# Hybrid decoder step on one core: two column groups take turns over the first blocks, with the loads and casts of the start reordered

## The chip, the cores and the metric

The kernel runs on one core of a Trainium2 chip. The metric is the device time of one execution in microseconds (us); lower is better. The time before the change is 1706.85 us, the median of 3 runs (1706.56 to 1708.28).

## The reference, cut to what matters

One layer of a decoder trunk is computed for 256 prompt tokens and 32 sample tokens (8 sequences of 4). The vectors `x` of all 288 tokens (width 2048) meet one wide input projection; its columns feed a short gated convolution and a gated delta-rule mixer. Both results are merged, projected, normalised, and pass through a two-matrix feed-forward part.

```python
proj = x @ w_in                                   # 2048 -> 11280 columns
conv_out, new_conv_a = causal_depthwise_conv(gC * h, conv_a_buf, conv_a_w)
y_a = (gB * conv_out) @ w_a_out
qkv, new_gdn_buf = causal_depthwise_conv(concat([q, k, v]), gdn_buf, gdn_conv_w)
o, S = gated_delta_rule(l2norm(q), l2norm(k), v, g, beta, S0)   # q, k, v after silu
y_b = gated_rmsnorm(o, z) @ w_b_out
x = layer_norm(ALPHA * x + (sig(m_a) * y_a + sig(m_b) * y_b) @ w_o)
x = layer_norm(ALPHA * x + square(relu(x @ w_up)) @ w_down)
```

The sample tokens bring histories: the last convolution inputs of each sequence (`state_conv_a`, `state_gdn_conv`) and the delta-rule state. Everything is in 32-bit floats.

## The kernel before, in words

**Blocks.** Every product with a weight matrix is cut into *column groups* of 256 output columns, and each group into *blocks* of 512 rows of the weight matrix. A block is one DMA of 512 KB (`load`, L164, on SP's queue, into a tile `raw`, 4 buffers). To keep accuracy, each weight and each activation is split into a rounded part and a rest: `split_hi` (L173) casts `raw` to `hi` on ScalarE, `split_lo` (L179) computes `lo` = `raw` - `hi` on VectorE, and `matmuls` (L186) issues 24 matmuls for the block: 4 row tiles, 2 column tiles, and for each the *triple* hi by xh (L202), hi by xl (L203), lo by xh (L204). `hi` and `lo` have 4 buffers each. A group's 4 blocks (with 2048 rows) accumulate in one of two PSUM tiles `acc`; after the group's last block an *evacuation* is spread over the following blocks by `at(...)`.

**Order.** The program writes the order of each engine out by hand; an engine runs its instructions in program order. The main loop (L1309) does, for each block i: the cast `hi` of block i+3 (`AHEAD` = 3), one step of the side work, `lo` of block i+3, the evacuations that are due, the matmuls of block i, and the load of block i+7. While `matmuls` runs, one entry of the list `fill` is emitted after each triple.

**The start.** The first blocks multiply by `x`, which must first be turned: tokens stand on partitions in DRAM's order, and the matmuls want features on partitions. `x` comes as four *parts* of 512 features (`xr[i]`, L715 to L718), prompt (512 KB) and sample tokens (64 KB) by separate DMAs, each followed by `load(i)`, all on SP's queue. `x_tile(k)` (L732) turns 128 features: two transposes of 128x128 for the prompt, a small one for the 32 sample tokens, then a cast to `xh` on ScalarE and the rest `xl` on VectorE. Part 0 is turned before block 0; the tiles of part i+1 are the `fill` of block i (i = 0, 1, 2), and `hi` and `lo` of block i+1 are emitted just ahead of block i. Ahead of all this, 8 bf16 matmuls on a zeroed tile `warm` are issued (L708). The histories, convolution weights and three gain vectors are loaded into `hwr`, `har` (16 DMAs on POOL's queue, from the beginning) and `lnr` (SP's queue), and turned by `hist_tiles` (L741) ahead of block 4. The constants `cf`, `cfe`, `ci`, and `wbar`, `arow` are loaded on SP's queue behind block 4's load (L1285 to L1293).

**The first 24 blocks** are the six groups k, k, q, q, v, v of the delta-rule's first four heads (`conv_evac`, L249). Group 0 has blocks 0 to 3, group 1 blocks 4 to 7. The evacuation of a group has two pieces on successive blocks, each with copies out of PSUM on ScalarE (L263, L264), a multiplication (L266), three fused steps on VectorE (L268) and two small POOL copies, and then a step `last` with the SiLU.

**The side work** is a generator: `gates()` (from block 4), then the delta rule `gdn(0)` (from block 20 at the earliest) and `gdn(1)`, one step per block; a second generator `sample()` runs beside it. Its instructions stand between those of the blocks on every engine.

Of the kernel before, what the change touches and what calls it, by code (L numbers as in the profile page):

```python
# [103 lines left out]
def hybrid_kernel(ctx: ExitStack, tc: tile.TileContext, A):  # L104
# [15 lines left out]
    def nm(s):  # L120
        counter[0] += 1
        return f"{s}{counter[0]}"

    def gtile():
        n = nm("g")
        return gp.tile([P, 512], F32, tag="g", name=n)
# [12 lines left out]
    def tt(out, a, b, op):  # L139
        dve.tensor_tensor(out=out, in0=a, in1=b, op=op)  # L140
# [23 lines left out]
    def load(i):  # L164
        if i >= len(blocks):
            return
        gi, r0, k0, _, _ = blocks[i]
        t = wp.tile([P, KB, GW], F32, tag="raw", name=nm("raw"))
        sp.dma_start(t, gi["W"][r0:r0 + KB * P, gi["col0"]:gi["col0"] + GW]
                     .rearrange("(k p) c -> p k c", p=P))  # L170
        raw[i] = t
# [77 lines left out]
    def conv_evac(sec, G, p):  # L249
        def piece(t):  # L250
            hh = 2 * p + t
            ti = sec * 8 + 4 * G + hh
            tl = {}

            def f(ps):
                gpool = gd["pool"]
                w1 = gpool.tile([P, 640], F32, tag="w1", name=nm("w1"), bufs=2)
                pad, cv = w1[:, 0:320], w1[:, 320:640]
                tl["cv"] = cv
                sm = pad[:, 259:315].rearrange("p (b s) -> p b s", s=7)  # L260
                gps.memset(pad[:, 0:3], 0.0)
                gps.tensor_copy(sm[:, :, 0:3], hw[:, ti, 0:24].rearrange("p (b j) -> p b j", j=3))
                act.copy(pad[:, 3:259], ps[:, t, 0:NP_])  # L263
                act.copy(sm[:, :, 3:7], ps[:, t, NP_:NT].rearrange("p (b s) -> p b s", s=4))  # L264
                c = cv[:, 0:312]
                act.mul(c, pad[:, 0:312], hw[:, ti, 24:25])  # L266
                for j in range(1, 4):
                    stt(c, pad[:, j:j + 312], hw[:, ti, 24 + j:25 + j], c, MUL, ADD)  # L268
                gps.tensor_copy(stB[:, ti, :].rearrange("p (g j) -> p g j", j=3),
                                pad[:, 256:319].rearrange("p (g s) -> p g s", s=7)[:, :, 0:3])  # L270

            def f2(ps):
                cv = tl["cv"]
                cs = cv[:, 259:315].rearrange("p (b s) -> p b s", s=7)[:, :, 0:4]
                if sec == 2:
                    act.activation(gd["v", G][:, hh // 2, :, hh % 2, :],
                                   cv[:, 0:NP_].rearrange("p (c x) -> p c x", c=4), AF.Silu)
                    act.activation(gd["vs", G][:, hh], cs, AF.Silu)
                else:
                    side_ = hh % 2 if sec == 1 else 1 - hh % 2  # L280
                    act.activation(gd["kq", G][:, hh, :, side_, :],
                                   cv[:, 0:NP_].rearrange("p (c x) -> p c x", c=4), AF.Silu)
                    act.activation(gd["kqs", G][:, 1 - sec, hh], cs, AF.Silu)
            return f, f2
        (a0, a1), (b0, b1) = piece(0), piece(1)

        def last(ps):
            a1(ps)
            b1(ps)
        return [a0, b0, last]  # L290

    mark = {}
    for G in range(2):
        mark["kqv", G] = len(blocks)
        for sec, c0 in ((1, C_K), (0, C_Q), (2, C_V)):
            for p in range(2):
                add_group(w_in, c0 + 512 * G + GW * p, 0, KT, acts_x, conv_evac(sec, G, p))
        mark["kqv_end", G] = len(blocks)

    def h_evac(p):  # L300
        def f(ps):
# [403 lines left out]
    warm = tx.tile([P, 512], mybir.dt.bfloat16, name="warm")  # L705
    dve.memset(warm, 0.0)
    wps = gtile()
    for _ in range(8):  # L708
        pe.matmul(wps, warm[:, 0:P], warm, start=True, stop=True)
    xr = [tx.tile([P, 3, 512], F32, name=f"xr{i}") for i in range(4)]  # L710
    xpr = A["x_prompt"][0].rearrange("(b p) f -> p b f", p=P)
    xsr = A["x_sample"].rearrange("b t f -> (b t) f")
    sp.dma_start(cf[:, 0:128], A["cf"][:, 0:128])
    for i in range(4):
        c = slice(512 * i, 512 * i + 512)  # L715
        sp.dma_start(xr[i][:, 0:2, :], xpr[:, :, c])
        sp.dma_start(xr[i][0:NS, 2, :], xsr[:, c])
        load(i)  # L718
    hwr = tx.tile([112, 768], F32, name="hwr")
    har = tx.tile([76, 256], F32, name="har")  # L720
    for g in range(4):
        c, c2 = slice(768 * g, 768 * g + 768), slice(256 * g, 256 * g + 256)
        gps.dma_start(hwr[28 * g:28 * g + 24, :], A["state_gdn_conv"][0].rearrange("b j c -> (b j) c")[:, c])
        gps.dma_start(hwr[28 * g + 24:28 * g + 28, :], A["gdn_conv_w"][0][:, c])
        gps.dma_start(har[19 * g:19 * g + 16, :], A["state_conv_a"][0].rearrange("b j c -> (b j) c")[:, c2])
        gps.dma_start(har[19 * g + 16:19 * g + 19, :], A["conv_a_w"][0][:, c2])
    lnr = tx.tile([33, P], F32, name="lnr")
    gps.memset(epsc[:, 0:1], LN_EPS)
    gps.memset(epsc[:, 1:2], NORM_EPS)
    gps.memset(epsc[:, 2:3], 1.28e-10)  # L730

    def x_tile(k):  # L732
        i, kk = k // 4, k % 4
        g = gtile()
        for b in range(2):
            pe.transpose(g[:, b * P:(b + 1) * P], xr[i][:, b, kk * P:(kk + 1) * P], ident)  # L736
        pe.transpose(g[:, NP_:NT], xr[i][0:NS, 2, kk * P:(kk + 1) * P], ident[0:NS, 0:NS])
        act.copy(xh[:, k, :], g[:, 0:NT])
        tt(xl[:, k, :], g[:, 0:NT], xh[:, k, :], SUB)

    def hist_tiles():  # L741
        g = gtile()
# [529 lines left out]

    cur = [0]
    aux = []
    his[0] = wp.tile([P, KB, GW], F32R, tag="hi", name=nm("hi"))
    los[0] = wp.tile([P, KB, GW], F32R, tag="lo", name=nm("lo"))
    t = raw.pop(0)
    for k in range(KB + 2):
        if k < KB:
            x_tile(k)  # L1280
        if k > 1:
            act.copy(his[0][:, k - 2], t[:, k - 2])  # L1282
            tt(los[0][:, k - 2], t[:, k - 2], his[0][:, k - 2], SUB)
    load(4)
    sp.dma_start(cf[:, 128:], A["cf"][:, 128:NE])  # L1285
    sp.dma_start(cfe, A["cf"][:, NE:NL])
    sp.dma_start(ci, A["ci"])
    sp.dma_start(lnr[0:16, :], A["ln1_g"].rearrange("o (k p) -> (o k) p", p=P))
    sp.dma_start(lnr[16:32, :], A["ln1_b"].rearrange("o (k p) -> (o k) p", p=P))
    sp.dma_start(lnr[32:33, :], A["gdn_norm_w"])  # L1290
    sp.dma_start(wbar, w_in[:, C_BA:C_BA + 16].rearrange("(k p) c -> p k c", p=P))
    sp.dma_start(arow[:, 0, :], A["a_log"].to_broadcast([P, 8]))
    sp.dma_start(arow[:, 1, :], A["dt_bias"].to_broadcast([P, 8]))  # L1293
    for i in range(3):
        split_hi(i + 1, 2)
        split_lo(i + 1, 2)
        load(i + 5)
        fill.extend(lambda k=k: x_tile(k) for k in range(4 * i + 4, 4 * i + 8))
        matmuls(i)
    for i in range(4, AHEAD + 3):  # L1300
        split_hi(i)
        split_lo(i)
        load(i + 4)
    sgen = side()
    gcm = None
    for p in range(8):
        for n, f in enumerate(residual1(p)):
            at(mark["up"] + 6 + 4 * p + n, f)
    for i in range(3, len(blocks)):  # L1309
        cur[0] = i  # L1310
        split_hi(i + AHEAD)
        if i == 4:
            hist_tiles()
            tx_cm.__exit__(None, None, None)
            gcm = tc.tile_pool(name="gdn", bufs=1)
            gpool = gcm.__enter__()
            gd["pool"] = gpool
            for G in range(2):
                gd["kq", G] = gpool.tile([P, 4, 4, 2, 64], F32, tag="kq", name=f"kq{G}", bufs=2)
                gd["kqs", G] = gpool.tile([P, 2, 4, 8, 4], F32, tag="kqs", name=f"kqs{G}", bufs=2)  # L1320
                gd["v", G] = gpool.tile([P, 2, 4, 2, 64], F32, tag="vf", name=f"vf{G}")
                gd["vs", G] = gpool.tile([P, 4, 8, 4], F32, tag="vfs", name=f"vfs{G}")
        if i > 3 and sgen:
            if i == mark["merge"]:
                for _ in sgen:
                    pass
                sgen = None
            else:
                next(sgen, None)
                if aux and next(aux[0], aux) is aux:  # L1330
                    aux.pop(0)
            if i == mark["conv"] + 1:
                gd["ao"] = ap_.tile([P, 2, H, NT], F32, tag="ao", name="ao")
# [24 lines left out]
            tail_consts()  # L1358
        matmuls(i)
        load(i + AHEAD + 4)  # L1360
    for i in sorted(due):
        for f in due[i]:
            f()
# [30 lines left out]
```

## Time and profile before

| what | value |
|---|---|
| median of 3 runs | 1706.85 us (1706.56 to 1708.28) |
| the profiled execution's own time | 1707.81 us |
| its span, first to last instruction | 1706.0 us |
| mean granted TensorE clock | 0.992 |
| TensorE busy (matmul) | 99% of the span |
| VectorE, ScalarE, GpSimd busy | 59%, 43%, 8% |
| DMA moved | 279.69 MB, mean 164 GB/s |

The device time of the profiled execution is 1.81 us longer than its span. "Busy" for TensorE counts an instruction from start to modelled end, so a matmul at half clock counts as busy. Rows of the timeline read: start in us, duration in us, engine, source line, operation, tile written <- tiles read, shape, count, and in brackets how long the engine had been idle and what released it. PE is TensorE, PEld its weight load, ACT ScalarE, DVE VectorE, POOL GpSimd, SP the engine whose queue issues most DMAs; SPq and POOLq are the issuing queues.

### The profile page before, as it was taken

What the parts mean: (1) busy time and instruction counts of PE and PEld (TensorE: products, weight loads), DVE (VectorE), ACT (ScalarE), POOL (GpSimd) and SP (SyncE); (2) the same over time, 40 slices, a digit from 0 to 9 for tenths busy, and PEclk for the clock granted to TensorE, in tenths of its full rate; (3) what the DMA queues carried; (4) which work ended last, traced back from release to release, by engine and by line L of the source; (5) the groups of instructions that cost most, each with busy time, mean ns of one, the idle gap of its engine ahead of it and who ended that gap; (6) DMA issues with size and microseconds to landing.
All of it is one profiled execution on the core that took longest, in us unless ns stands there. A gap on an engine that the chain in (4) does not pass through costs nothing.

```text
span 1706.0 us, 31049 instructions
## 1 busy us (share of the span) xinstructions
PE 1688.2 (99%) x13045; PEld 1668.4 (98%) x13045; DVE 1012.1 (59%) x1301; ACT 726.6 (43%) x1052; POOL 132.4 (8%) x221
## 2 busy tenths in 40 slices
PE   9999999999999999999999999999999999999997
PEld 7999999999999999999999999999999999999996
DVE  5577876758544445456778844565445654466575
ACT  5675626333543333334445533344334433344331
POOL 2232412023300000000010000000000000000000
PEclk8999999999999999999999999999999999999998
DMA  8464356435555555555565555555555555555552
GB/s 251 140 187 148 112 174 200 151 113 180 164 170 170 162 165 169 161 170 163 160 194 175 170 164 167 166 162 167 166 162 160 171 164 169 163 162 160 174 158 72
DMA packets 272295, 279.69 MB, mean 164 GB/s; under 512 B 12122, under 2 KB 267035, under 8 KB 272023
## 3 DMA queue, kind: packets, MB, share of 16 engines
q1 hardware_dynamic: 267324, 265.80, 50.1%
q0 software_dynamic: 4256, 11.65, 2.4%
q8 instruction: 102, 1.67, 0.4%
q10 hardware_dynamic: 576, 0.26, 0.1%
q14 instruction: 37, 0.30, 0.1%
HBM read 270.19 MB, written 7.48 MB: 163 GB/s over the span
## 4 chain that ended last, share of the span: by engine, by line
PE 98%; DVE 1%; DMA 0%; POOL 0%; issue 0%; SPq 0%; ACT 0%
PE acc L202 31%; PE acc L203 31%; PE acc L204 31%; PE g L1022 1%; DMA xr<-in_x_prompt_dram 0%; PE g L1010 0%; PE g L1169 0%; PE g L1189 0%; PE g L769 0%; DVE w L143 0%; PE g L1192 0%; PE g L1141 0%; PE g L1181 0%; PE g L736 0%; PE g L591 0%; PE g L896 0%
## 5 line engine op out<-in xcount | busy, mean ns | idle before, releaser
L140 DVE TENSOR_TENSOR lo<-raw,hi 128x1024 fp32r<-128x1024 f32 (+2 forms) x502 | 613.9, 1226 | 554.1 <-ACT hi L177 551.2
L177 ACT CAST hi<-raw 128x1024 fp32r<-128x1024 f32 (+1 forms) x498 | 517.4, 1041 | 768.1 <-PE acc L203 710.9
L202 PE MATMUL acc<-xh,hi 128*128 128x288 f32 x1408 | 423.3, 301 | 0.4 <-ACT hi L1282 0.4
L204 PE MATMUL acc<-xh,lo 128*128 128x288 f32 x1408 | 416.9, 296 | 0.0
L203 PE MATMUL acc<-xl,hi 128*128 128x288 f32 x1408 | 416.9, 296 | 0.0
L202 PE MATMUL acc<-dh,hi 128*128 128x290 f32 x1024 | 303.9, 297 | 0.0
L203 PE MATMUL acc<-dl,hi 128*128 128x290 f32 x1024 | 303.3, 296 | 0.0
L204 PE MATMUL acc<-dh,lo 128*128 128x290 f32 x1024 | 302.7, 296 | 0.0
L204 PE MATMUL acc<-hh,lo 128*128 128x288 f32 x1024 | 302.3, 295 | 0.0
L203 PE MATMUL acc<-hl,hi 128*128 128x288 f32 x1024 | 302.3, 295 | 0.0
L202 PE MATMUL acc<-hh,hi 128*128 128x288 f32 x1024 | 302.2, 295 | 0.0
L202 PEld LDWEIGHTS acc<-xh,hi 128*128 128x128 f32 x1408 | 265.8, 189 | 3.0 <-issue 0.7
L203 PEld LDWEIGHTS acc<-xl,hi 128*128 128x128 f32 x1408 | 266.3, 189 | 0.5
L204 PEld LDWEIGHTS acc<-xh,lo 128*128 128x128 f32 x1408 | 265.9, 189 | 0.0
L202 PEld LDWEIGHTS acc<-dh,hi 128*128 128x128 f32 x1024 | 193.6, 189 | 0.1
L204 PEld LDWEIGHTS acc<-dh,lo 128*128 128x128 f32 x1024 | 193.3, 189 | 0.0
L203 PEld LDWEIGHTS acc<-dl,hi 128*128 128x128 f32 x1024 | 193.3, 189 | 0.1
L203 PEld LDWEIGHTS acc<-hl,hi 128*128 128x128 f32 x1024 | 192.5, 188 | 0.0
L204 PEld LDWEIGHTS acc<-hh,lo 128*128 128x128 f32 x1024 | 192.3, 188 | 0.0
L202 PEld LDWEIGHTS acc<-hh,hi 128*128 128x128 f32 x1024 | 192.1, 188 | 0.0
L203 PE MATMUL acc<-ml,hi 128*128 128x288 f32 x256 | 75.6, 295 | 0.0
L204 PE MATMUL acc<-mh,lo 128*128 128x288 f32 x256 | 75.6, 295 | 0.0
(390 smaller groups left out, 1611.9 us busy)
## 6 DMA issues: line engine op xcount, KB each, us to landing
raw<-in_w_in_dram SPq DMA_DIRECT2D x176, 512.0 KB, 3.5
raw<-in_w_up_dram SPq DMA_DIRECT2D x128, 512.0 KB, 3.7
raw<-in_w_down_dram SPq DMA_DIRECT2D x128, 512.0 KB, 3.6
raw<-in_w_o_dram SPq DMA_DIRECT2D x32, 512.0 KB, 3.7
raw<-in_w_a_out_dram SPq DMA_DIRECT2D x16, 512.0 KB, 3.6
raw<-in_w_b_out_dram SPq DMA_DIRECT2D x16, 512.0 KB, 3.6
S<-in_state_gdn_dram POOLq DMA_DIRECT2D x8, 512.0 KB, 7.6
out_dram<-S POOLq DMA_DIRECT2D x8, 512.0 KB, 5.0
```

The source lines that it names most:

```text
L140: dve.tensor_tensor(out=out, in0=a, in1=b, op=op)
L177: act.copy(his[i][:, k:k + step], raw[i][:, k:k + step])
L202: pe.matmul(o, wh, xh_, start=st, stop=False)
L203: pe.matmul(o, wh, xl_, start=False, stop=False)
L204: pe.matmul(o, wl, xh_, start=False, stop=en)
L1022: pe.matmul(out[r, q * 64:q * 64 + 64], a[r, q, :], b[r, q, :], start=True, stop=True)
```

## The change

1. **Block order.** The first eight blocks alternate between groups 0 and 1: the two blocks that need part 0 of `x`, then the two that need part 1, and so on. Group 0 now ends at block 6 and group 1 at block 7; both `acc` tiles are in use from block 1. The evacuation of group 0 does both pieces in one step.
2. **x.** Each part is turned by `x_steps`: for two feature tiles of the prompt four transposes and one cast and one rest of 2x256 columns; for the sample tokens of all four feature tiles a single 128x128 transpose. Part 0 before block 0; parts 1, 2, 3 in the `fill` of blocks 1, 3, 5. The sample tokens come by four DMAs on ACT's queue at its very beginning.
3. **Loads.** SP's order is now `cf`, part 0 in two halves, blocks 0 and 1, part 1, blocks 2 and 3, parts 2 and 3, blocks 4 to 6. The constants follow the loads of blocks 9 to 12.
4. **Histories.** POOL first makes a one-element copy that reads part 2 of `x`, then issues the 16 DMAs and the three of `lnr`. `hist_tiles` moves ahead of block 6.
5. **Order of the splits.** `hi` and `lo` of blocks 0, 1, 2 ahead of block 0, and from there the loop's rule, i+3 ahead of block i, so `hi` of block 4 stands ahead of part 1's casts on ScalarE.
6. **Others.** 14 bf16 matmuls in place of 8. The side work starts at block 10 in place of 4.

```diff
+        def pair(ps):
+            a0(ps)
+            b0(ps)
+        if G == 0 and sec == 1 and p == 0:
+            return [pair, last]
         return [a0, b0, last]
...
+    blocks[0:8] = [blocks[4 * (u % 2) + u // 2] for u in range(8)]
...
-    for _ in range(8):
+    for _ in range(14):
         pe.matmul(wps, warm[:, 0:P], warm, start=True, stop=True)
...
-    for i in range(4):
-        c = slice(512 * i, 512 * i + 512)
-        sp.dma_start(xr[i][:, 0:2, :], xpr[:, :, c])
-        sp.dma_start(xr[i][0:NS, 2, :], xsr[:, c])
-        load(i)
+    for j in range(4):
+        act.dma_start(xs4[32 * j:32 * j + 32], xsr[:, :, j, :])
+    sp.dma_start(cf[:, 0:128], A["cf"][:, 0:128])
+    for u in range(2):
+        sp.dma_start(xr[0][:, :, 256 * u:256 * u + 256], xpr[:, :, 256 * u:256 * u + 256])
+    load(0)
+    load(1)
+    for i in range(1, 4):
+        sp.dma_start(xr[i], xpr[:, :, 512 * i:512 * i + 512])
+        if i == 1:
+            load(2)
+            load(3)
...
+    gps.tensor_copy(hwr[0:1, 0:1], xr[2][0:1, 0, 0:1])
...
-    def x_tile(k):
...
+    def x_steps(i):
+        def prompt(u):
...
+            def turn(k, b):
+                c = (2 * u + k) * P
+                return lambda: pe.transpose(gv[:, k, b * P:(b + 1) * P], xr[i][:, b, c:c + P], ident)
+
+            def out():
+                ks = slice(4 * i + 2 * u, 4 * i + 2 * u + 2)
+                act.copy(xh[:, ks, 0:NP_], gv)
+                tt(xl[:, ks, 0:NP_], gv, xh[:, ks, 0:NP_], SUB)
...
+        def sample():
...
+            return [lambda: pe.transpose(g[:, 0:P], xs4[:, i, :], ident)], out
...
-    for k in range(KB + 2):
-        if k < KB:
-            x_tile(k)
...
-    for i in range(3):
-        split_hi(i + 1, 2)
-        split_lo(i + 1, 2)
-        load(i + 5)
-        fill.extend(lambda k=k: x_tile(k) for k in range(4 * i + 4, 4 * i + 8))
-        matmuls(i)
...
+    for f in x_steps(0):
+        f()
+    split_hi(0, 2)
+    split_lo(0, 2)
...
+    for i in range(1, AHEAD):
+        split_hi(i, 2)
+        split_lo(i, 2)
+    for i in range(4, AHEAD + 4):
+        load(i)
...
-    for i in range(3, len(blocks)):
+    for i in range(len(blocks)):
         cur[0] = i
         split_hi(i + AHEAD)
-        if i == 4:
+        if i in (1, 3, 5):
+            a_, b_, c_ = x_steps(i // 2 + 1)
+            idle = lambda: None
+            fill.extend([idle, idle, idle, a_, b_, idle, c_])
+        if i == 6:
             hist_tiles()
...
-        if i > 3 and sgen:
+        if i > 9 and sgen:
...
         matmuls(i)
         load(i + AHEAD + 4)
+        if 2 <= i < 6:
+            rest[i - 2]()
```

More of the change, by code (lines that the diff above doesn't have):

```diff
@@ L707, in hybrid_kernel @@
     wps = gtile()
-    for _ in range(8):
+    for _ in range(14):
         pe.matmul(wps, warm[:, 0:P], warm, start=True, stop=True)
-    xr = [tx.tile([P, 3, 512], F32, name=f"xr{i}") for i in range(4)]
+    xr = [tx.tile([P, 2, 512], F32, name=f"xr{i}") for i in range(4)]
+    xs4 = tx.tile([P, 4, P], F32, name="xs4")
     xpr = A["x_prompt"][0].rearrange("(b p) f -> p b f", p=P)
-    xsr = A["x_sample"].rearrange("b t f -> (b t) f")
-    sp.dma_start(cf[:, 0:128], A["cf"][:, 0:128])
-    for i in range(4):
-        c = slice(512 * i, 512 * i + 512)
-        sp.dma_start(xr[i][:, 0:2, :], xpr[:, :, c])
-        sp.dma_start(xr[i][0:NS, 2, :], xsr[:, c])
-        load(i)
+    xsr = A["x_sample"].rearrange("b t (i j f) -> (b t) i j f", j=4, f=P)
     hwr = tx.tile([112, 768], F32, name="hwr")
     har = tx.tile([76, 256], F32, name="har")
+    lnr = tx.tile([33, P], F32, name="lnr")
+    for j in range(4):
[10 more added lines that the diff above has]
+            load(3)
+    gps.memset(epsc[:, 0:1], LN_EPS)
+    gps.memset(epsc[:, 1:2], NORM_EPS)
+    gps.memset(epsc[:, 2:3], 1.28e-10)
+    gps.tensor_copy(hwr[0:1, 0:1], xr[2][0:1, 0, 0:1])
     for g in range(4):
@@ L726, in hybrid_kernel, with out, step, f @@
         gps.dma_start(har[19 * g + 16:19 * g + 19, :], A["conv_a_w"][0][:, c2])
[L727 to L730, printed above, removed]
-    def x_tile(k):
[L733 to L739, printed above, removed]
+    gps.dma_start(lnr[0:16, :], A["ln1_g"].rearrange("o (k p) -> (o k) p", p=P))
+    gps.dma_start(lnr[16:32, :], A["ln1_b"].rearrange("o (k p) -> (o k) p", p=P))
+    gps.dma_start(lnr[32:33, :], A["gdn_norm_w"])
+    def x_steps(i):
+        def prompt(u):
+            g = gtile()
+            gv = g.rearrange("p (k t) -> p k t", k=2)
+            steps = []
+            def turn(k, b):
[5 more added lines that the diff above has]
+                tt(xl[:, ks, 0:NP_], gv, xh[:, ks, 0:NP_], SUB)
+            return [turn(k, b) for k in range(2) for b in range(2)], out
+        def sample():
+            g = gtile()
+            gv = g[:, 0:P].rearrange("p (k t) -> p k t", k=4)
+            def out():
+                ks = slice(4 * i, 4 * i + 4)
+                act.copy(xh[:, ks, NP_:NT], gv)
+                tt(xl[:, ks, NP_:NT], gv, xh[:, ks, NP_:NT], SUB)
+            return [lambda: pe.transpose(g[:, 0:P], xs4[:, i, :], ident)], out
+        def step(part):
+            def f():
+                turns, out = part()
+                for g in turns:
+                    g()
+                out()
+            return f
+        return [step(lambda: prompt(0)), step(sample), step(lambda: prompt(1))]
     def hist_tiles():
@@ L1274, in hybrid_kernel @@
     aux = []
-    his[0] = wp.tile([P, KB, GW], F32R, tag="hi", name=nm("hi"))
-    los[0] = wp.tile([P, KB, GW], F32R, tag="lo", name=nm("lo"))
-    t = raw.pop(0)
-    for k in range(KB + 2):
-        if k < KB:
-            x_tile(k)
[L1281 to L1293, printed above, removed]
-    for i in range(3):
-        split_hi(i + 1, 2)
-        split_lo(i + 1, 2)
-        load(i + 5)
-        fill.extend(lambda k=k: x_tile(k) for k in range(4 * i + 4, 4 * i + 8))
-        matmuls(i)
[L1300 to L1303, printed above, removed]
+    for f in x_steps(0):
+        f()
+    split_hi(0, 2)
+    split_lo(0, 2)
+    rest = [lambda: sp.dma_start(cf[:, 128:], A["cf"][:, 128:NE]),
+            lambda: sp.dma_start(cfe, A["cf"][:, NE:NL]),
+            lambda: sp.dma_start(wbar, w_in[:, C_BA:C_BA + 16].rearrange("(k p) c -> p k c", p=P)),
+            lambda: (sp.dma_start(ci, A["ci"]),
+                     sp.dma_start(arow[:, 0, :], A["a_log"].to_broadcast([P, 8])),
+                     sp.dma_start(arow[:, 1, :], A["dt_bias"].to_broadcast([P, 8])))]
+    for i in range(1, AHEAD):
[3 more added lines that the diff above has]
+        load(i)
     sgen = side()
```

## The prediction

> **What bounds the kernel now.** I read the page's busy line first, then the list of TensorE's waits, then the timeline and the windows of the first 35 us. The page:
>
> ```profile
> span 1706.0 us, 31049 instructions
> PE 1688.2 (99%) x13045; PEld 1668.4 (98%) x13045; DVE 1012.1 (59%) x1301; ACT 726.6 (43%) x1052; POOL 132.4 (8%) x221
> ```
>
> TensorE bounds the whole: only 17.8 us of 1706 are not busy. What a change of the first blocks can bring is therefore what TensorE loses there, in waits or at a low clock, which counts as busy. Its waits over the whole span, longest first:
>
> ```profile
> PE g L1141 <- DVE E L143: 3.0, 1, 3.0
> PE g L637 <- DVE R L140: 2.6, 1, 2.6
> PE g L736 <- DMA xr<-in_x_prompt_dram: 2.2, 2, 1.2
> ```
>
> The second belongs to the end, which the change leaves alone. The third is the start, the first the side work near 213 us, which the change moves by one block. The windows (length, then busy us of PE, PEld, DVE, ACT, POOL, granted clock, DMA share, GB/s) show what is larger than the waits:
>
> ```profile
> 0.00:8.32 8.32, 5.81 (x20) 2.38 (x20) 1.59 (x4) 2.85 (x6) 5.74 (x15) 1.00 0.73 215
> 8.32:18.56 10.24, 8.92 (x32) 6.98 (x33) 5.58 (x14) 4.76 (x13) 2.90 (x9) 0.50 1.08 291
> 18.56:33.40 14.84, 14.84 (x102) 13.17 (x101) 8.71 (x14) 7.07 (x13) 0.00 (x0) 1.00 0.92 251
> ```
>
> From 8.32 to 18.56 the clock is half, and DMA is full (share 1.08 at 291 GB/s). On the timeline:
>
> ```profile
> 10.73 0.66 PE L736 MATMUL g<-cf,xr 128*128 128x128 f32 x2 [1.24 <-DMA xr<-in_x_prompt_dram]
> 16.62 0.61 PE L202 MATMUL acc<-xh,hi 128*128 128x288 f32 x1
> 19.43 0.30 PE L204 MATMUL acc<-xh,lo 128*128 128x288 f32 x1
> 19.57 0.38 PE L736 MATMUL g<-cf,xr 128*128 128x128 f32 x2
> 20.06 0.40 PE L202 MATMUL acc<-xh,hi 128*128 128x288 f32 x1
> 30.26 0.30 PE L202 MATMUL acc<-xh,hi 128*128 128x288 f32 x1
> 33.45 0.55 PE L744 MATMUL g<-cf,hwr 112*128 112x112 f32 x4
> ```
>
> Block 3 runs from 30.26 to 33.45: **3.19 us a block** at full clock. A tile of x costs 20.06 - 19.43 - 0.13 = 0.5 us or more inside a block. Four blocks alone are 12.8 us, but they and all of x are done only at 33.45. So 20.7 us is the start's overhead; no change of the start can bring more than a part of it.
>
> **The change part by part.** I ask when the same work (four blocks, 16 tiles of x turned) is done afterwards, against 33.45. The histories' turning costs the same before block 6 as before block 4.
>
> *Turning x.* Where four 128x128 transposes follow each other:
>
> ```profile
> 1681.39 0.30 PE L204 MATMUL acc<-hh,lo 128*128 128x288 f32 x1
> 1681.52 0.60 PE L591 MATMUL g<-cf,acc 128*128 128x128 f32 x4
> 1681.88 0.38 PE L202 MATMUL acc<-hh,hi 128*128 128x288 f32 x1
> ```
>
> they take 0.36 us, 0.09 each. A part of x is now 9 of them: 0.8 us, with three breaks in the row of matmuls about 1.0 us, in place of 4 tiles of 0.5 to 0.6. This saves 1.2 us a part.
>
> *The first two blocks.* Eight warming matmuls take 3.60 us:
>
> ```profile
> 1.19 3.60 PE L709 MATMUL g<-warm 128*128 128x512 bf16 x8 [1.19 <-DVE warm L706]
> 5.78 0.41 PE L736 MATMUL g<-cf,xr 128*128 128x128 f32 x2 [0.99 <-DMA xr<-in_x_prompt_dram]
> 13.36 1.14 ACT L177 CAST hi<-raw 128x512 fp32r<-128x512 f32 x2 [3.79 <-DMA raw<-in_w_in_dram]
> 14.01 1.29 DVE L140 TENSOR_TENSOR lo<-raw,hi 128x512 fp32r<-128x512 f32 x2 [3.83 <-ACT hi L177]
> 28.97 2.94 ACT L177 CAST hi<-raw 128x1024 fp32r<-128x1024 f32 x3
> 30.05 3.50 DVE L140 TENSOR_TENSOR lo<-raw,hi 128x1024 fp32r<-128x1024 f32 x3 [0.49 <-ACT hi L177]
> ```
>
> Fourteen end between 6 us (the last six at double clock) and 7.2 us. Part 0 has landed by then (transposes began at 5.78 before, with more bytes ahead). Then 4 transposes, three casts and the first half of `hi` on ScalarE (0.57 us per 512 columns), and on VectorE the rests and `lo` (0.65): block 0 is in full run 3.5 us later, at 9.5 to 10.7. Blocks 0 and 1 end at 17 to 18 us at full clock, at about 22 at half.
>
> *The new wait, which decides.* Block 2 needs part 1 of x. Part 1, awaited till 10.73 before, has 704 KB more ahead of it (512 + 256 of block 1 and the sample tokens, less their first 64), lands by 13 us at 300 GB/s (below) and is turned in block 1. But its casts stand on ScalarE behind `hi` of block 4 (emitted at the head of block 1), and its rests on VectorE behind `lo` of block 4. Both engines go in order, so part 1 **waits for block 4's weights to land**, and behind it everything on ScalarE: `hi` of blocks 5 and 6 too. On SP's queue block 4 comes after all of x. In the trace of before (the first row is two issues, the second that block's KB and us to landing):
>
> ```profile
> 10.61 1.00 SPq L169 DMA_DIRECT2D raw<-in_w_in_dram  x2
> raw<-in_w_in_dram SPq DMA_DIRECT2D x1, 512.0 KB, 10.7
> 6.00:16.00 10.00, 8.35 (x34) 5.96 (x33) 5.16 (x13) 4.89 (x13) 4.21 (x11) 0.62 1.07 300
> 16.00:22.00 6.00, 6.00 (x34) 5.01 (x32) 3.03 (x7) 2.23 (x5) 0.00 (x0) 0.79 1.08 335
> ```
>
> Block 4 landed at 11.1 + 10.7 = 21.8 us. Ahead of it, with itself, were 64 + 4 x (512 + 64 + 512) + 512 = 4928 KB on SP. Afterwards: 64 + 2048 + 5 x 512 on SP and 256 on ACT, 4928 KB again. What leaves are the histories, 412 KB, 1.4 us at 300 GB/s; about a third returns once part 2 has landed (1024 KB, 3.4 us, ahead of block 4: near 17 us; +0.5), and the sample tokens use the slack DMA has before 6 us (-0.2). So 20.7 us; bounds 19.4 (335 GB/s throughout) and 21.8 (as before). The Trainium skill (DMA: Bandwidth & Descriptors, Issuing engines are not separate DMA queues) says that transfers of all issuing engines share the 16 DMA engines and only issue time is saved; the DMA share of 1.08 agrees, and a queue of its own for the 256 KB would bring the landing 0.9 us forward.
>
> From there: `hi` of block 4 0.98 (21.7), `lo` 1.17 (22.85), the rest of part 1's first pair 0.65 and of the sample tokens, an estimate from the 0.65 for 512 columns, 0.3: **block 2 in full run at 23.8**. Then two blocks 6.4, and parts 2 and 3, 1.0 each: 32.2 against 33.45, **-1.25 us**.
>
> *The clock.* TensorE then stands still for some 5 us before block 2 (none to 2 us if blocks 0 and 1 were at half clock). The trace shows the clock fall at 8.32, 3.5 us after the last warming matmul, with only transposes between, and return at 18.56. So block 2 starts at half clock. Till the return: 1.9 us (matmuls ran without a break from 16.62) to 7.8 us (from 10.73); I take 4, nearer to the first since block 2 has no breaks, and half of that is lost: **+2.0 us** (bounds 1.0 and 3.9). The Trainium skill (TensorE: Matmul & The Clock Gate, What's actually happening and Part 4: PE-mode transpose) names a free-running window of 3.413 us and says transposes don't count as busy; 10.24 us is three such windows, and by it the loss would be 1.7 to 3.4.
>
> *The evacuations.* Blocks 6 and 7 now end groups in a row, and block 8 needs group 0's `acc`. One piece on ScalarE and VectorE:
>
> ```profile
> 37.79 1.05 ACT L177 CAST hi<-raw 128x1024 fp32r<-128x1024 f32 x1 [0.96 <-PE acc L203]
> 38.75 0.36 ACT L263 COPY w<-acc 128x256 f32<-128x256 f32 x1
> 39.01 0.19 ACT L264 COPY w<-acc 128x32 f32<-128x32 f32 x1
> 39.30 0.56 ACT L266 ACTIVATE w<-w,hw 128x312 f32<-128x312 f32 x1
> ```
>
> After block 6: cast 1.05, piece 1.1, the second's two copies 0.45: 2.6, within block 7's 3.19. Nothing, with 0.5 us to spare; without that cover, up to 0.5.
>
> *Histories and constants.* POOL issued 16 DMAs in 12.4 us:
>
> ```profile
> 1.29 0.70 POOL L723 DMA_DIRECT2D hwr<-in_state_gdn_conv_dram  x1 [0.84 <-POOLq L1381]
> 13.17 0.51 POOL L726 DMA_DIRECT2D har<-in_conv_a_w_dram  x1
> hwr<-in_state_gdn_conv_dram POOLq DMA_DIRECT2D x4, 72.0 KB, 6.2
> ```
>
> Now 19 from 17 us: 14.7 and 6.2 to land, 37.9. Block 6 comes at 32.2 + 2.0 + 6.4 = 40.6. Hidden with 2.7 us to spare. Behind POOL's new wait stand only these DMAs and later the pieces' copies. The constants' loads on SP sit behind weights that are needed three blocks later; nothing. The gates' matmuls only change places.
>
> *The side work.* The gates take eleven steps; from block 10 they end at block 20, so `gdn(0)` starts at block 21 in place of 20, and all its steps move by one block against the evacuations. The wait of 3.0 us:
>
> ```profile
> 204.78 2.75 POOL L1130 TENSOR_TENSOR vm<-v,cf 128x1024 fp32r<-128x1024 f32 x1 [8.86 <-PE g L1181]
> 207.52 1.16 POOL L262 COPY w<-hw 128x24 f32<-128x24 f32 x1
> 209.31 2.87 DVE L143 SCALAR_TENSOR_TENSOR w<-w,hw 128x312 f32<-128x312 f32 x3 [0.69 <-ACT w L266]
> 214.85 1.12 DVE L143 SCALAR_TENSOR_TENSOR E<-E,gexp,g 128x128 f32<-128x128 f32 x4
> ```
>
> The state update at 214.85 frees the PSUM that TensorE waits for. It is late because the evacuation piece at 209.31 waited through ScalarE for POOL's copy behind its 2.75 us product. Moved by a block, the same VectorE work stands between, but only the second piece meets that product: the 0.69 idle goes and a little of the slowing. **-0.9 us**, bounds -3.0 (the wait gone) and +3.5 (below).
>
> *Sum*: -1.25 + 2.0 - 0.9 = -0.15 us on the profiled execution: 1707.66. That execution is 0.96 above the median of the runs shown, so **1706.7**.
>
> **The rivals.**
> *The clock holds or returns at once* (blocks 0 and 1 at half clock fill the gap), or block 4 lands at 19.4: the sum loses 2.0, or 1.3, or both: 1704.7, 1705.4, 1703.4; with the wait at 213 us gone, 2.1 less, down to 1701.3. For it: the clock's return can't be placed. Against: 5 us of idleness if block 0 starts at full clock.
> *The hold doesn't bite*, because DMA is faster without the small transfers of the start: then block 0 at 9.75, four blocks and three parts end at 25.5, and the histories become the wait: ready at 30 to 37.9 against block 6 at 31.9, block 6 begins 7.9 to 1.9 us sooner than before's 40.8 (33.45, two blocks, and about 1.0 for the histories' turning, which is in both); with the side's 0.9 that is 1698.0 to 1704.1. Against it: 4.9 MB by 16 us would take over 400 GB/s from 4 us on; the windows show 300 to 335.
> *Slower: the moved side work.* At block 51 the state update comes behind both pieces, three `lo` and three POOL products. The rows above show 2.87 where a piece's three steps alone take 1.70:
>
> ```profile
> 37.33 1.70 DVE L143 SCALAR_TENSOR_TENSOR w<-w,hw 128x312 f32<-128x312 f32 x3
> ```
>
> If each product slows VectorE by 1.2, three of them make the wait 3.0 + 3.5 and not 2.1; it decides once VectorE is over one block (3.2 us) behind at block 51. In place of -0.9 stands +3.5: 1711.1.
>
> **How the numbers follow.** The forecast, 1706.7, has 0.45 (its own range 1704.4 to 1708.7, from the bounds of the landing and the clock); the clock or an early landing 0.25; no hold 0.14; the moved side work 0.16. About 0.2% (3.4 us) is what a measurement of this kernel can tell from no change. Faster, below 1703.4: most of no hold, over half of the clock case where its parts add up, 0.30. Slower, above 1710.3: 0.15. Within: 0.55. The range leaves out the lower part of no hold and most of the moved side work: 1701.0 to 1710.0.
>
> **What would show it.** Right: ScalarE's cast of block 4 released by a DMA near 21 us, `xh` of part 1 right behind it, TensorE idle some 5 us ahead of block 2, the granted clock at half after it; the histories' turning without a wait; a wait at L1141 near 2 us. Wrong: block 2 begun before 20 us; `hi` of block 4 released by TensorE; TensorE waiting for `hwr`; new waits of TensorE on VectorE in the side work.

## The result and the profile after

The changed kernel takes 1712.99 us (median of 6 runs, 1711.61 to 1715.26) against 1707.87 us of the kernel before beside it: a ratio of 1.0028, 95% interval [1.0019, 1.0038]. It is **slower by about 5 us** (0.3%), above the range of the prediction. The profiled execution took 1712.01 us. Its page begins:

```profile
span 1710.2 us, 31024 instructions
PE 1684.9 (99%) x13039; PEld 1667.6 (98%) x13039; DVE 1013.1 (59%) x1294; ACT 726.1 (42%) x1045; POOL 128.4 (8%) x225
```

TensorE is busy 3.3 us less than before, yet the span is 4.2 us longer: its idle time grows from 17.8 to 25.3 us. TensorE's waits, longest first (who waited, for whom, us in total, times, longest):

```profile
PE g L964 <- POOL vmh L960: 3.4, 1, 3.4
PE g L1187 <- DVE E L143: 3.3, 1, 3.3
PE g L644 <- DVE R L140: 2.6, 1, 2.6
PE g L776 <- DMA xs<-in_x_sample_dram: 2.2, 1, 2.2
...
PE acc L202 <- ACT hi L177: 1.2, 1, 1.2
PE acc L203 <- DVE xl L140: 1.0, 1, 1.0
PE acc L202 <- ACT xh L774: 0.8, 1, 0.8
```

L1187 is the old wait near 213 us (L1141 in the kernel before; the lines have moved): 3.3 for 3.0. The first row is new. It is the turning of the delta rule's replicated sample keys, which waits for a copy on POOL. The windows (same columns as before) give its place, and the clock:

```profile
0.00:11.46 11.46, 6.61 (x26) 3.07 (x26) 2.62 (x6) 4.12 (x7) 0.37 (x7) 1.00 0.79 250
11.46:14.88 3.42, 3.42 (x14) 3.42 (x15) 2.39 (x5) 1.81 (x4) 0.00 (x0) 0.50 1.07 364
14.88:35.00 20.12, 18.31 (x140) 17.86 (x139) 10.44 (x14) 8.58 (x12) 10.68 (x20) 1.00 0.94 284
35.00:104.10 69.10, 69.09 (x528) 67.73 (x526) 40.56 (x68) 46.07 (x102) 18.17 (x45) 1.00 0.55 155
104.10:107.45 3.35, 0.00 (x0) 0.00 (x0) 2.97 (x5) 3.30 (x7) 1.54 (x1) 0.94 0.86 253
107.45:110.50 3.05, 3.04 (x13) 3.04 (x14) 1.72 (x2) 3.00 (x9) 0.34 (x2) 0.51 0.59 182
```

At the start the clock is half for 3.4 us only, in place of 10.2. From 104.10 to 107.45 TensorE does nothing, and the 3.05 us behind that run at half clock, which loses another 1.5: **4.9 us** in all at this one place.

The start itself went better than forecast. Block 6, behind the histories' turning, begins on TensorE at 40.92 in the kernel before and here at 38.22. Three rows of ScalarE and one of TensorE (the second matmul of block 2) show the forecast wait:

```profile
19.38 1.05 ACT L177 CAST hi<-raw 128x1024 fp32r<-128x1024 f32 x1 [3.27 <-DMA raw<-in_w_in_dram]
20.33 0.58 ACT L764 CAST xh<-g 128x512 fp32r<-128x512 f32 x1
20.81 0.27 ACT L774 CAST xh<-g 128x128 fp32r<-128x128 f32 x1
```

```profile
22.53 0.40 PE L203 MATMUL acc<-xl,hi 128*128 128x288 f32 x1 [1.01 <-DVE xl L140]
```

The first matmul of block 6, in the kernel before and then here:

```profile
40.92 0.29 PE L202 MATMUL acc<-xh,hi 128*128 128x288 f32 x1
```

```profile
38.22 0.40 PE L202 MATMUL acc<-xh,hi 128*128 128x288 f32 x1
```

The cast of block 4 is released by a DMA at 19.38, the casts of part 1 stand right behind it, and block 2 is in full run at 22.5.

Where the new wait comes from is read on POOL, before and after. In the kernel before, the delta rule's first step (block 20, which starts at 92.6 us on TensorE) is four state loads and three fills, then the evacuation piece's copy at L262:

```profile
84.64 3.60 POOL L864 DMA_DIRECT2D S<-in_state_gdn_dram  x4
88.22 1.09 POOL L882 MEMSET b<- 128x1152 f32 x1
...
91.06 0.22 POOL L262 COPY w<-hw 128x24 f32<-128x24 f32 x1
```

They wait for nothing that other engines do then, and POOL, done with the copy of the piece before (83.78), has nothing else ahead of them: it runs them 8 us early, and the copy is there at 91 us. In the changed kernel:

```profile
94.61 0.19 POOL L879 COPY gsw<-qt 64x8 f32<-64x8 f32 x1
...
95.03 0.21 POOL L269 COPY stB<-w 128x27 f32<-128x27 f32 x1
95.18 3.59 POOL L910 DMA_DIRECT2D S<-in_state_gdn_dram  x4
98.76 1.08 POOL L928 MEMSET b<- 128x1152 f32 x1
...
101.59 0.21 POOL L262 COPY w<-hw 128x24 f32<-128x24 f32 x1
...
105.86 1.54 POOL L960 COPY vmh<-kqs 128x512 f32<-128x512 f32 x1 [3.92 <-DVE red L947]
```

The gates' last copies (94.61) and block 20's piece (95.03) stand ahead, so the 6.6 us begin only at 95.18, and block 21's copy comes at 101.59. ScalarE waits for it:

```profile
101.84 0.56 ACT L266 ACTIVATE w<-w,hw 128x312 f32<-128x312 f32 x1 [2.36 <-POOL w L262]
```

Behind that stand the squares of the keys, VectorE's sums of them, and, as they read the buffer that POOL's next copy writes, this copy (105.86), and TensorE.

### The profile page after: what moved, and what is told of

Read it like the earlier page. It is cut to its first block, busy times and chain, and to the rows that moved or that the text cites. A ratio compares the mean times of both kernels' runs of the same rounds, so it can differ in the third digit from the quotient of the medians.

```text
span 1710.2 us, 31024 instructions
## 1 busy us (share of the span) xinstructions
PE 1684.9 (99%) x13039; PEld 1667.6 (98%) x13039; DVE 1013.1 (59%) x1294; ACT 726.1 (42%) x1045; POOL 128.4 (8%) x225
## 4 chain that ended last, share of the span: by engine, by line
PE 91%; DVE 4%; ACT 2%; issue 1%; DMA 1%; POOL 1%; ACTq 0%; DVEq 0%; POOLq 0%
PE acc L202 29%; PE acc L203 29%; PE acc L204 29%; DVE lo L140 1%; DVE w L143 1%; PE g L1068 1%; ACT hi L177 1%; PE g L1056 0%; DMA raw<-in_w_in_dram 0%; DMA xs<-in_x_sample_dram 0%; PE g L815 0%; PE g L1235 0%; PE g L1187 0%; PE g L1215 0%; POOL S L910 0%
## 5 line engine op out<-in xcount | busy, mean ns | idle before, releaser
L140 DVE TENSOR_TENSOR lo<-raw,hi 128x1024 fp32r<-128x1024 f32 (+1 forms) x499 | 613.2, 1232 | 554.2 <-ACT hi L177 552.0
```

## The experiments

Two questions: what makes the side work slower (e1 to e4, e9), and what the start's parts are worth (e5, e7, e8, e11). Three more (e6, e10, e12) try what else the side work and the loads can give. Theory 1: the delta rule's first step is one block later, so its POOL work falls between the two pieces of an evacuation. Theory 2: the gates now end right ahead of it, so POOL can't run ahead. A third possibility was that the start itself costs the 5 us. Each is timed beside the kernel before (medians 1707.8 to 1708.5 us); the ratio and its 95% interval are to that.

**e1.** The side work from block 9:

```diff
-        if i > 9 and sgen:
+        if i > 8 and sgen:
```

> The changed kernel with the side work begun at block 9 in place of 10, so that the delta rule of the first heads begins at block 20 as before, right behind the gates. Theory 1 (place): the changed kernel is slower because the delta rule's first step at block 21 puts 6.6 us of POOL work (four state loads, three fills) between the POOL copies of the two evacuation pieces of blocks 20 and 21; at block 20 it stands ahead of both. Then the 3.4 us wait of TensorE at the turning of the sample keys and the 1.7 us at half clock behind it go: 1705 to 1708 us. Theory 2 (lateness): it is that the gates end right ahead of the delta rule, so POOL can't run ahead; then the wait stays: 1711 to 1713 us.

1714.35 us, 1.0039 [1.0026, 1.0051]. The wait is longer:

```profile
PE g L964 <- POOL vmh L960: 5.4, 1, 5.4
```

POOL begins the loads at 93.55, behind the gates' last copy, and gives the piece's copy at 100.11, 9 us later than the kernel before, though the order of the steps against the blocks is the old one. The time is above both forecasts, and theory 1 alone falls.

**e2.** From block 7, the delta rule at block 20 as before:

```diff
-        if i > 9 and sgen:
+        if i > 6 and sgen:
```

> The changed kernel with the side work begun at block 7: the gates end at block 17, the delta rule begins at block 20 after idle blocks, as before. Both theories: no wait at the turning of the sample keys, and the start's gain of about 3 us is left: 1704 to 1706.5 us. If a third cause in the start's change were at work, it stays near 1713.

1706.26 us, 0.9988 [0.9979, 0.9997]. No wait at L964. On POOL the loads run early again:

```profile
86.94 3.60 POOL L910 DMA_DIRECT2D S<-in_state_gdn_dram  x4
...
93.37 0.22 POOL L262 COPY w<-hw 128x24 f32<-128x24 f32 x1
```

So the start by itself gains 1.6 us (0.5 to 3.6 by the interval), and **the move of the side work costs 6.7 us** (1712.99 against 1706.26).

**e3.** The kernel before with the delta rule one block later:

```diff
-            while cur[0] < mark["kqv", G] + 20 or aux:
+            while cur[0] < mark["kqv", G] + 21 or aux:
```

> The kernel before, with one number changed: the delta rule of the first heads begins at block 21 at the earliest in place of 20. Nothing of the start is changed and the gates end at block 14. Theory 1 (place): the wait of 3 to 4 us and the half clock appear here too, 1711 to 1714 us. Theory 2 (lateness): POOL has run ahead, no wait, 1706 to 1709 us.

1710.29 us, 1.0013 [1.0005, 1.0022], between the two forecasts. Its POOL begins the loads at 95.38, behind a piece's copy, and gives the next at 101.80, as late as in the changed kernel; but TensorE doesn't wait at this place: it gets there only as the copy that it needs (L914, the same as L960) has ended, at 107.64.

```profile
106.09 1.55 POOL L914 COPY vmh<-kqs 128x512 f32<-128x512 f32 x1 [3.93 <-DVE red L901]
```

```profile
107.71 0.64 PE L918 MATMUL g<-cf,vmh 128*128 128x128 f32 x4
```

The wait near 213 us grows to 3.3, with three small ones (0.3, 0.2, 0.2) behind it.

**e4.** e2 with the same one-block shift.

> The changed kernel with the side work begun at block 7 but the delta rule at block 21. Theory 1 (place): as slow as the changed kernel, 1711 to 1714 us. Theory 2 (lateness): 1704 to 1707 us.

1708.10 us, 1.0001 [0.9992, 1.0011], 1.8 above e2 and above the forecast of theory 2, far below that of theory 1. The wait is there, but small:

```profile
PE g L964 <- POOL vmh L960: 0.8, 1, 0.8
```

Here POOL begins the loads at 93.87, 1.3 us earlier than in the changed kernel, and TensorE arrives later. So theory 2 has the larger part. By this path, of 6.7 us the shift by a block costs 1.8 and the gates' lateness on top of it 4.9; by the other path (e1) the lateness alone costs 8.1 (1714.35 against 1706.26), and the shift on top of it takes 1.4 back. The two don't simply add: what counts is when POOL's copy ends against when TensorE gets there.

**e9.** The changed kernel with nothing moved but the POOL work, into a step of the delta rule that was empty:

```diff
-        for hh in range(4):
-            gps.dma_start(S0[:, hh], A["state_gdn"][0, :, 4 * G + hh].rearrange("b d e -> d b e"))
-        gps.memset(kqm, 0.0)
-        for z in (U128, aT):
-            gps.memset(z, 0.0)
...
         tt(glx[:, 1], glf, glx[:, 0], SUB)
         yield
+        for hh in range(4):
+            gps.dma_start(S0[:, hh], A["state_gdn"][0, :, 4 * G + hh].rearrange("b d e -> d b e"))
+        gps.memset(kqm, 0.0)
+        for z in (U128, aT):
+            gps.memset(z, 0.0)
         yield
```

> The changed kernel as it is (side work from block 10, delta rule from block 21), with the delta rule's four state loads and three fills, 6.6 us of POOL, emitted five steps later, in a step that was empty. If POOL's queue is what delays the evacuation's copy and through it everything up to the turning of the sample keys: the 3.4 us wait and the half clock behind it go, 1706.5 to 1709 us. If the late gates delay ScalarE and VectorE by themselves: the wait stays, 1711 to 1713 us.

1709.60 us, 1.0008 [0.9999, 1.0017]: 3.4 us are back, a little less than forecast. The wait at this place (now L958) is 1.1 in place of 3.4, and a new one stands further on:

```profile
PE g L1067 <- DVE xt L1085: 1.4, 1, 1.4
...
PE g L958 <- POOL vmh L954: 1.1, 1, 1.1
```

The 2.3 us that are gone match the 2.36 us that ScalarE waited for POOL behind the loads and fills. What stays is behind the gates' last copies on POOL, which are about as late as in the changed kernel (94.16 against 94.61): the piece of block 20 waits for them, and the rest of the chain follows.

```profile
94.68 0.56 ACT L266 ACTIVATE w<-w,hw 128x312 f32<-128x312 f32 x1 [1.88 <-POOL w L262]
```

That this wait makes up the whole 1.1 was not tested. The seven profiled executions together, for the turning of the sample keys (us):

| kernel | POOL's copy ends | TensorE gets there | TensorE waits |
|---|---|---|---|
| before | 101.91 | 103.34 | 0 |
| e2 | 101.56 | 102.19 | 0 |
| e3 | 107.64 | 107.71 | 0 |
| e4 | 106.11 | 105.39 | 0.8 |
| e9 | 104.70 | 103.64 | 1.1 |
| changed | 107.40 | 104.09 | 3.4 |
| e1 | 106.39 | 101.10 | 5.4 |

**e5.** e2 without the *hold*, that is, the casts of part 1 standing behind the cast of block 4:

```diff
-        split_hi(i + AHEAD)
+        if i != 1:
+            split_hi(i + AHEAD)
...
         matmuls(i)
+        if i == 1:
+            split_hi(i + AHEAD)
+            split_lo(i + AHEAD)
```

(and the same condition at `split_lo`).

> The changed kernel with the side work at block 7, and the cast and rest of block 4 emitted behind the matmuls of block 1, so that part 1 of x no longer waits for block 4's weights. If that hold costs the start its time: the 2 to 3 us of waits ahead of block 2 go and the clock stays up, 1703 to 1704.5 us against 1706.3 with the hold. If DMA itself is the bound, block 3 or 4 waits in its place: 1705.5 to 1707 us.

1702.76 us, 0.9967 [0.9955, 0.9979]: 3.5 us below e2, a little more than forecast. The casts of part 1 follow their transposes, and those of blocks 4 and 5 come behind them:

```profile
17.78 0.59 ACT L764 CAST xh<-g 128x512 fp32r<-128x512 f32 x1 [1.97 <-PE g L760]
18.29 0.27 ACT L774 CAST xh<-g 128x128 fp32r<-128x128 f32 x1
...
20.01 2.00 ACT L177 CAST hi<-raw 128x1024 fp32r<-128x1024 f32 x2
```

No wait ahead of block 2 is left. The hold was real, and it, not DMA, set block 2's start.

**e7.** e2 with 8 warming matmuls (`range(14)` back to `range(8)`).

> The changed kernel with the side work at block 7 and 8 warming matmuls in place of 14. If the hold ahead of block 2 swallows what happens earlier: 1705.5 to 1707.5 us, as with 14. If the longer warming holds the clock up where it counts: 1708 us or more.

1705.12 us, 0.9981 [0.9971, 0.9990], a little below the first forecast; e2's own interval overlaps it. The six more matmuls bring nothing that can be measured. TensorE waits 3.1 us for the sample tokens in place of 1.6, and block 4's cast still starts at 19.43.

**e8.** e2 without POOL's copy that waits for part 2 (`gps.tensor_copy(hwr[0:1, 0:1], ...)` left out).

> The changed kernel with the side work at block 7, and POOL's copy that waits for part 2 of x left out, so that the histories' transfers run from the beginning again (the copy's element is overwritten by them, nothing of the result hangs on it). Their 412 KB then stand ahead of block 4's weights: block 2 starts 1 to 1.5 us later, 1707 to 1708 us. If they don't compete with the weights: 1706.3 us as before.

1710.01 us, 1.0007 [0.9998, 1.0015]: 3.8 above e2, more than forecast. Block 4's cast:

```profile
21.60 1.04 ACT L177 CAST hi<-raw 128x1024 fp32r<-128x1024 f32 x1 [3.17 <-PE acc L204]
```

It comes 2.3 us later than e2's 19.30. (The row names TensorE; block 0's matmuls were over by 17.4, so the other condition of this cast, the landing, is left as the releaser.) Keeping the histories back is worth more than any other load order tried here.

**e11.** e5 with the sample tokens' transfers on SP's queue, behind the first constants.

> The kernel of e5, with the four transfers of the sample tokens on SP's queue behind the first constants and ahead of the prompt's part 0, in place of ACT's queue. If ACT's queue is served beside SP's and so its 256 KB come late: the sample tokens land by 6 us in place of 8.7, block 0 starts 1 us sooner, 1701.5 to 1702.5 us. If a queue of its own is an advantage: part 0 and the weights come 1 to 2 us later, 1703 to 1705 us.

1705.67 us, 0.9986 [0.9977, 0.9995], but its runs spread from 1702.57 to 1708.87; the profiled one has the same span as e5's, 1700.8. The sample tokens are no longer awaited; TensorE waits 2.4 us for the first `hi` instead of 1.2. The time is above both forecasts. ACT's queue is not worse, by the medians it is better. The four executions with a granted clock of 0.992 took 1706.58 to 1708.87, the other seven (0.994 or 0.995) 1702.57 to 1706.48; what sets the spread stays open.

**e6.** e5 with the delta rule from block 19 (`+ 20` to `+ 19`).

> The same with the delta rule of the first heads from block 19 in place of 20. If the 3.0 us wait near 213 us hangs on how the side work stands to the evacuations, it shrinks or grows and nothing else: 1699 to 1703 us if it goes with its half clock (up to 4.7 us), 1703 to 1704.5 if it stays.

1713.23 us, 1.0030 [1.0019, 1.0042]: 10.5 us slower than e5 for one block. The expectation was wrong. The waits between 34 and 470 us:

```profile
PE g L1235 <- DVE v L140: 2.9, 1, 2.9
PE g L1215 <- DVE E L143: 2.3, 1, 2.3
PE g L942 <- ACT kq L281: 2.3, 1, 2.3
PE g L795 <- DMA lnr<-in_gdn_norm_w_dram: 2.1, 1, 2.1
PE g L1187 <- DVE E L143: 1.5, 1, 1.5
```

The first step now comes before the SiLU of its keys is done (L942), and new waits come further on. That they come from the steps meeting other evacuations was not tested. The fourth row is the last small load behind the histories. It can be late once the hold is gone: e5's profile doesn't have this wait, e10's and e11's do (2.4 and 1.0).

**e10.** e5 with one empty step in the sample generator (a second `yield` behind `spread(0)`), to see what the old 3 us near 213 us were.

> The kernel of e5 (1702.8 us), with one empty step more in the sample generator, so that its pair of state products stands one block behind the delta rule's state update and not in the same block. If the 3.0 us wait near 213 us is for one of four PSUM tiles, of which five are asked for in that block: the wait and the half clock behind it go, 1698 to 1700 us. If it is VectorE being behind altogether, it moves on by a block: 1702 to 1704 us.

1701.32 us (1698.44 to 1702.57), 0.9955 [0.9943, 0.9968]. The wait goes from 3.0 to 0.3:

```profile
PE g L795 <- DMA lnr<-in_gdn_norm_w_dram: 2.4, 1, 2.4
...
PE g L1188 <- DVE E L143: 0.3, 1, 0.3
```

That it goes, and doesn't move on by a block, is what the theory of the four PSUM tiles forecast. The time is between the two forecasts: the median falls by 1.4 us, and the intervals of e5 and e10 overlap. This profile, unlike e5's, waits 2.4 us for the last small load behind the histories, and runs at half clock from 36.89 to 40.30 behind it.

**e12.** e10 with the three small loads of the gain vectors (`lnr`) on ACT's queue at the beginning.

> The kernel of e10 with the three small loads of the gain vectors on ACT's queue at the beginning, behind the sample tokens, in place of POOL's queue behind the histories. In e10 TensorE waits 2.4 us for the last of them ahead of block 6. If the histories proper are in time: that wait goes, 1698.5 to 1700.5 us. If they are as late themselves, or the loads at the start delay part 0: 1701 to 1703 us.

1699.10 us (1697.94 to 1700.05), 0.9946 [0.9932, 0.9959]: the fastest, 9 us below the kernel before. No wait for the histories is left in its profile; the wait at the sample tokens of the start is 2.0 (0.8 in e5, 1.7 in e10).

## Why the prediction was wrong, point by point

*What failed: the term of the side work*, -0.9 us, and the sentence that "the gates' matmuls only change places". Measured by e2 against the changed kernel, the move costs **6.7 us**. Against the kernel before, the forecast was +0.75 for the start and -0.9 for the side work; the runs give -1.6 and +6.7, together the 5.1 us that were measured. The prediction saw that the gates end at block 20 and the delta rule starts at block 21, and then looked only at the wait that the trace of before already had, at 213 us; there it forecast a wait near 2 us in place of 3.0, and 3.3 was measured. It did not ask what the first moved step issues. Its loads and fills, 6.6 us of POOL, were in the trace of before, but at 84.64, where they cost nothing because POOL ran ahead. The gap between the gates' end and block 20 had been their cover. e2 gives the cover back; e9 takes the POOL work out of the way and gets 3.4 of the 6.7 us back; e1 shows that the gates' lateness alone is enough for the loss, e4 that the shift alone is not. The slower rival blamed the right part, the moved side work, but by another mechanism (VectorE slowed by POOL's products) and in another place: block 51, not blocks 21 to 24. That its 1711.1 is nearest to 1712.99 is luck.

*The wait for block 4's weights* was right: a cast released by a DMA at 19.38, where 20.7 was forecast with 19.4 as the early bound, the casts of part 1 behind it, block 2 in full run at 22.53 (forecast 23.8). e5 shows its worth, 3.5 us. The landing was 1.3 us earlier than forecast. e8 points to the histories: with them at the beginning the cast comes 2.3 us later, where the prediction took 1.4 off for them and put 0.5 back.

*The clock*, +2.0 us, was wrong in this execution: the half clock fell on blocks 0 and 1 (11.46 to 14.88), which ended at 20.3, so TensorE stood still for no more than 2 us and block 2 ran at full clock. It is the rival's picture. In e2's execution block 2 was slowed from 23.25 to 26.67 us:

```profile
24.00:25.00 1.00, 1.00 (x6) 1.00 (x5) 0.13 (x1) 0.00 (x0) 0.91 (x3) 0.50 1.12 249
```

Block 6 begins there at 39.66, 1.4 us later than in the changed kernel's execution. So the term is real but comes and goes between executions. (The upper end of the forecast's own range, 1708.7, doesn't follow from its bounds: 1.1 for the landing and 1.9 for the clock give 1709.7. Both are below what was measured.)

*Turning x* (four transposes in 0.36 us) and *the evacuations* (no wait at blocks 7 to 10) were right. *The histories* were in time, block 6 at 38.2 and no wait; that they would become the wait if the hold went was right in e6 and e10, not in e5's own profile.

*What is not settled*: why e3 and e4 lose 1.8 to 2.4 us when at the turning of the sample keys they wait 0 and 0.8. Their profiled executions lose more near 213 us than the wait itself: the half clock behind it lasts two stretches of 3.4 us in place of one. In e3, then in the kernel before:

```profile
219.42:226.25 6.83, 5.11 (x20) 5.01 (x21) 5.64 (x9) 1.26 (x3) 2.77 (x2) 0.50 0.56 173
```

```profile
216.52:219.94 3.42, 3.42 (x17) 3.42 (x16) 2.87 (x3) 0.00 (x0) 2.66 (x2) 0.50 0.08 23
```

e4 shows the same (218.00 to 224.83, against 214.40 to 217.81 in e2). That is up to 1.7 us each, and in e3 the waits there sum to about 1 us more. But both took longer than the medians of their kernels (1711.26 and 1709.98), and nine of e3's eleven had a higher granted clock (0.992 to 0.996 against 0.990) and still took 1709.8 to 1710.8 us. So for the medians the question stays open.

## What to carry to other kernels

When generated side work is moved, list everything its first steps issue on every engine, and look in the old trace when those instructions ran, not when they were needed: work that ran ahead in a gap has no row among the waits, and loses its cover silently. A cast that is emitted early for a later block holds all casts behind it until its data lands; the order within one engine should follow the order in which data arrives. And time a change of order together with its parts apart: here a gain of 1.6 us and a loss of 6.7 were in one diff.

## What the runs showed of the hardware that was not expected

The stretches at half clock last 3.4 us or a multiple of it: 3.42 here (11.46 to 14.88), 10.24 in the kernel before, 13.65 in e3 (7.80 to 21.45). In e2 the clock fell at 23.25, after a stretch of that length in which TensorE was busy for 1.20 us; in e4 it fell at 23.44, after one with 1.52. In the changed kernel the stretches around the wait ahead of block 2, with 2.42 and 2.60 us, kept it. The rows of e2 and of the changed kernel:

```profile
19.84:23.25 3.41, 1.20 (x7) 0.98 (x8) 2.88 (x5) 2.59 (x5) 2.03 (x5) 1.00 1.02 276
```

```profile
18.30:21.72 3.42, 2.42 (x18) 1.98 (x16) 1.26 (x2) 2.34 (x5) 3.42 (x8) 1.00 1.09 348
21.72:25.13 3.41, 2.60 (x19) 2.60 (x20) 2.49 (x4) 0.79 (x1) 1.35 (x4) 1.00 0.94 230
```

So TensorE need not be idle for the whole stretch to lose the clock: one filled to about a third was lost. A threshold doesn't follow: earlier in e2 (6.19 to 9.60) a stretch with 1.80 us, most of it transposes, kept the clock. The Trainium skill (TensorE: Matmul & The Clock Gate, What's actually happening) has the window's length, 3413 ns, and that it is free-running, which the differing phases of these executions agree with; it speaks of an idle window, where here a partly busy one sufficed.

The four transfers of the sample tokens, 64 KB each, were issued on ACT's queue from 0.74 us, and TensorE waited for them until 8.70, though part 0 of the prompt, issued later on SP's queue, was turned at 5.92.
